# Residual of group 0 loaded by range, two pools exchanged, and head 0's operands on GpSimd's queue

## The chip, the cores and the metric

One core of a Trainium2 chip. The time is the device time of one execution in microseconds (us). Engines: TensorE (PE; its weight loads PEld), VectorE (DVE), ScalarE (ACT), GpSimd (POOL) and SyncE (SP), which here only issues DMAs. ACT and POOL can issue DMAs too, each in its own instruction order.

## The reference

One layer of a hybrid encoder for two requests, a prompt of 1024 rows and a sample of 32 rows, with the same weights (1056 rows together):

```python
h = x * (1 + sc1) + sh1                      # sc, sh, g: adaLN, silu(c) @ w_ada
mq, mk, mv, mo, mi, mf, fq, fk, fv, ff, gu, gv = split(h @ w_in)
hm = head_norm(mlstm(mq, mk, mv, mi, mf)) * norm_g * sigmoid(mo)     # 4 heads
hf = forgetting_attention(fq, fk, fv, log_sigmoid(ff))               # FoX, 8 heads
hg = gu * spatial_gate(layer_norm(gv))                               # gMLP
mix = concat([hm, hf, hg]) @ w_o
x = layer_norm(ALPHA * x + (1 + g1) * mix)
h = x * (1 + sc2) + sh2
y = (silu(h @ w_gate) * (h @ w_up)) @ w_down
x = layer_norm(ALPHA * x + (1 + g2) * y)
```

Outputs are x for both requests and the new states, the keys and values of the attention among them.

## The kernel before

The 1056 rows lie on the free axis (feature-major) and are worked in two groups: group 0 is rows 0 to 511, group 1 the other 544. Every fp32 product is made of three matmuls of a split operand: high times high (L116), high times low (L117), low times high (L118). A weight of 128 x 1024 comes in by SP as `raw` (512 KB, three buffers), ACT copies its high part (`whi`, L104), and DVE subtracts to get the low part (`wlo`, L105). `load` (L84) issues on SP and remembers the instruction as `lastload`; `store` issues on SP unless it is told another engine.

The instructions are written out in Python in one order, and a scheduler that simulates the engines then sets the order on each engine. Pools are stacks at two ends of SBUF; when one is closed, what is opened over its space waits, tile by tile, for the last reader of the old tile. `issue_after` holds what is issued in it behind an instruction that is named.

The order of work around the change, in `run`:

1. `wo_mix(0)` loads and splits the mixed heads of group 0 (`tm_ah`, `tm_al`), with feature-major units (`fm_unit`) for some heads of group 1 in between. Such a unit computes a head's queries and keys, stores them in DRAM (`start_dqh`, `start_dql`), and stores the keys as an output (`o_kT<-fm_qkr`), the last of them from ACT's queue.
2. `wo_res(0)` allocates `z0`, group 0's residual (in the trace `wo_z`), and loads it in four loads of 512 KB.
3. `wo_range` makes the output projection for rows 0 to 255 (range 0), then for rows 256 to 511 (range 1); for each block m of 128 features there are one weight and 24 matmuls 256 wide, after which DVE adds the product to `z0` (L1066). Range 1 is woven with `ln1` of range 0, and `ln1` of range 1 follows. `ln1` normalises `z0` in place on DVE, ACT writes the modulated value, and copy and difference (L1091, L1092) overwrite `tm_ah` and `tm_al`, the operands of the up projection.
4. `fm_unit` for the last heads; `ln1_res(0)` (L1094, POOL L1101) scales `z0` once more for the second residual: 16 instructions 128 x 256.
5. The stack `s1` with the pools `p1` (operands h1 of the input projection) and `sm` (small tiles, `fm_qkr` among them) is closed, and `mx1` is opened over their space for the mixers of group 1: `fox` for heads 0 to 7 (with k1, k2, qp, q2, v loaded by SP, L747 to L755) and `mlstm` units. The mLSTM unit loads `mqk`, `mqb`, `mv1`, `mo`, `mb`; ACT makes the sigmoid of `mo` in three steps (L607 to L609) and POOL multiplies it (L610); DVE and ACT make the weights `mw` from `mb` (L615, L618).
6. `up` (gate and up projection with silu, L1139 to L1145) of group 0, woven with the mixers, and `ada` (the adaLN product of a block of w_ada in four columns of PE, a copy `ada_adas` on ACT at L181, and two transposes of it on PE at L184).

Of the kernel before, what the change touches and what calls it, by code (L numbers as in the profile page):

```python
# [7 lines left out]
F32 = mybir.dt.float32  # L8
# [7 lines left out]
P = 128  # L16
D = 1024
KT = 8
# [5 lines left out]
GO = (0, 512)  # L24
GN = (512, 544)
QD = 2
MM = (((0, 256), (256, 512)), ((0, 272), (272, 544)))
# [36 lines left out]
def f(ap):  # L64
    return ap.bitcast(F32)


class Kernel:
# [12 lines left out]
        kw = {} if bufs is None else {"bufs": bufs}  # L81
        return pool.tile(shape, dt, tag=tag, name=f"{self.phase}_{tag}_{self.n}", **kw)

    def load(self, out, in_):  # L84
        self.lastload = self.nc.sync.dma_start(out, in_)
        return self.lastload

# [290 lines left out]
                    nc.gpsimd.tensor_copy(self.qks[:, h, :], kr[:, n - NS:n])  # L378
        return evac

    def decay(self, out, h, rows, tiles):
        j0, j1 = tiles
        self.load(f(out).rearrange("p (j q) -> p j q", q=P),
                  self.dfs.rearrange("(j h) r q -> h r j q", h=8)[h, rows, j0:j1])

    def head_tiles(self, h, nq, nk):
        b = self.foxbufs
# [349 lines left out]
    def fox(self, h, chunks):  # L737
        self.phase = "fox"
        mx = self.mx
        q0, q1 = chunks[0][0] * P, (chunks[-1][-1] + 1) * P  # L740
        nq, nk, nb = q1 - q0, q1, q1 // P
        if h in self.heads:
            k1, k2, qp, q2, v = self.heads.pop(h)
        else:
            k1, k2, qp, q2, v = self.head_tiles(h, nq, nk)
            qs = slice(q0, q1)
            self.load(f(qp[0:64]), self.dqh[h, 0:64, qs])  # L747
            self.load(f(qp[64:128]), self.dql[h, 0:64, qs])
            self.load(f(k1[0:64]), self.dqh[h, 64:128, :nk])
            self.load(f(k1[64:128]), self.dqh[h, 64:128, :nk])  # L750
            self.load(f(q2[0:64]), self.dqh[h, 0:64, qs])
            self.decay(q2[64:68], h, slice(2, 6), (chunks[0][0], nb))
            self.load(f(k2[0:64]), self.dql[h, 64:128, :nk])
            self.decay(k2[64:68], h, slice(0, 4), (0, nb))
            self.load(f(v), self.dv[:, :nb, h * P:(h + 1) * P])  # L755
        for tiles in chunks:
            o = tiles[0] * P - q0
            n = len(tiles) * P
            yield from self.fox_chunk(h, tiles, nk, n, k1, k2, qp[:, o:o + n], q2[:, o:o + n], v)
# [251 lines left out]
                nc.scalar.copy(h, r)  # L1011
                nc.vector.tensor_tensor(self.hl[c][a][:, k, :b - a], r, f(h), ALU.subtract)

    def wo_res(self, c, pool):
        z = self.z[c] = self.t(pool, [P, KT, GN[c]], F32, f"z{c}", 1)
        for k in range(0, KT, 2):
            self.load(z[:, k:k + 2], self.d["xT"][k:k + 2, :, GO[c]:GO[c] + GN[c]].rearrange("k p n -> p k n"))

    def wo(self, c, st, cuts, eng, res=None):
        self.phase = f"wo{c}"  # L1020
# [22 lines left out]
    def wo_range(self, st, a, b, order, kept, pool):  # L1043
        nc, ko = self.nc, self.KORDER[0]
        hh, hl = self.hh[0][a], self.hl[0][a]
        st["order"] = order
        for m in order:
            self.phase = "wo0"
            w = kept.get(m) or self.weights(self.d["w_o"][m], KT, P, None, pool if m < 3 else None)
            kept[m] = w  # L1050
            ps = self.t(self.pg, [P, 512], F32, "g")
            self.gemm(ps[:, :b - a], [w[k] for k in ko], slice(0, P), lambda i: hh[:, ko[i], :b - a],
                      lambda i: hl[:, ko[i], :b - a])
            self.sublayer_end(0, self.z[0], m, ps, "g1", st, a, b)
            yield
# [109 lines left out]
    def sup_operand(self, ks):  # L1165
# [7 lines left out]
        def load(k):  # L1173
# [5 lines left out]
            return x, y  # L1179

        loaded = {k: load(k) for k in ks[:2]}
        yield
        for k in ks:
            self.phase = "sup"
            x, y = loaded.pop(k)
            tt(y[:, b], y[:, b], x[:, b], ALU.subtract)
            tt(x[:, b], x[:, a], x[:, b], ALU.subtract)
            tt(x[:, a], y[:, b], x[:, a], ALU.add)
            tt(y[:, a], x[:, a], y[:, a], ALU.subtract)
            for z, (h, l) in zip((x, y), self.T):  # L1190
                nc.scalar.copy(h[:, k], z)
                tt(l[:, k], z, f(h[:, k]), ALU.subtract)
            if k + 2 in ks:
                loaded[k + 2] = load(k + 2)
            yield
# [141 lines left out]
    def run(self):  # L1337
        nc, tc, d = self.nc, self.tc, self.d
# [25 lines left out]
        self.constants()  # L1364
        self.ph = self.pool("ph")
        s1 = ExitStack()
        self.p1 = self.pool("p1", ctx=s1, side="right")
        self.sm = self.pool("sm", 2, ctx=s1, side="right")
        self.h1t = [self.wide_tiles(), [self.t(self.p1, [P, KT, GN[1]], F32R, x) for x in ("h1h", "h1l")]]
        self.hs = self.t(self.p1, [P, KT, 2 * NS], F32R, "hs")  # L1370
        self.G = self.t(self.p1, [P, 9, 16], F32, "G")
# [84 lines left out]
        for h in range(QD, PRE):  # L1456
            self.fm_unit(w3[2 + h], self.evac_qk(h), (1,))
        self.wo_mix(0, self.KORDER[0][6:])
        self.wo_res(0, self.pz)
        self.pn = self.pool("pn")  # L1460
        self.ln_consts()
        st = self.ln_begin(nc.vector)
# [6 lines left out]
        weave(self.ln1(0, st, *MM[0][1]))  # L1469
        for h in range(PRE, 8):  # L1470
            self.fm_unit(w3[2 + h], self.evac_qk(h, True), (1,))
        self.ln1_res(0)
        s1.close()
        s4 = ExitStack()
        self.mx = self.pool("mx1", ctx=s4, side="right")
        self.foxbufs = (2, 1, 1, 1, 2)
        self.mixers()
        s5 = ExitStack()
        pa = self.pool("pa0", ctx=s5)
        self.pu, self.utag = self.pg, "gg"  # L1480
# [74 lines left out]
        n = nj * 256  # L1555
# [3 lines left out]
        for half, (a, b) in enumerate(LN[1][::-1]):  # L1559
# [6 lines left out]
            else:  # L1566
                h, l = (self.t(pb, [P, KT * 272], F32R, f"{x}{a}", 1) for x in ("ah", "al"))
# [117 lines left out]
```

## Time and profile before

| | |
|---|---|
| time, median of 3 runs | 1366.96 us (1365.69 to 1368.74) |
| the profiled execution | 1366.61 us, span 1364.7 us, mean granted clock 0.995 |
| PE busy | 1330.3 us, 97% of the span |
| DVE, ACT, POOL busy | 995.4, 656.7, 226.6 us |
| DMA | 221.70 MB, mean 162 GB/s |

The span runs from the first to the last instruction of the trace; the profiled execution's own time is 1.9 us longer. A row of the timeline gives start, duration, engine, source line, operation, the tiles as out<-in with their buffer numbers left out, the number of instructions in the row, and in brackets the idle time before them and what ended it. A row of the list of waits gives the time waited in total, how often, and the longest. A row of the windows gives the length of the stretch, busy time and instructions of PE, PEld, DVE, ACT and POOL, then the granted clock of PE, the busy share of the DMA engines and the GB/s.

### The profile page before, as it was taken

To read this page: it belongs to the slowest core of one execution; us is meant where nothing else is said; L and a number is where in the kernel's file an instruction comes from. 1 tells how busy PE (TensorE), PEld (TensorE's weight loads), DVE (VectorE), ACT (ScalarE), POOL (GpSimd) and SP (SyncE) were. 2 spreads that over 40 slices of the span, in tenths; PEclk is the share of its full clock that TensorE was granted. 3 is DMA by queue.
4 is the path that set the end of the run, shared out by engine and by line. 5 is a ranking of instruction groups with operands and counts; after the bars stand their busy time and mean duration, and the time that the engine had idled before them with its cause. 6 is when DMAs were issued, how large, how long until landed. Compare 5 with 4: busy or idle time off the path is not lost.

```text
span 1364.7 us, 25185 instructions
## 1 busy us (share of the span) xinstructions
PE 1330.3 (97%) x9434; PEld 1215.8 (89%) x9434; DVE 995.4 (73%) x2129; ACT 656.7 (48%) x1306; POOL 226.6 (17%) x263
## 2 busy tenths in 40 slices
PE   7999999999999899999999999999999999999996
PEld 4898889998989777888887888999999999999995
DVE  5545553679769667786776765678988988879777
ACT  3314454545536554545545354336664554645355
POOL 0202000053134200000000000373710000000341
PEclk9999999999999899999999999999999999999998
DMA  9765565547454765454344334574596758454321
GB/s 359 273 231 152 161 206 154 163 138 212 134 201 135 207 189 171 119 154 134 109 122 120 104 110 130 156 181 124 164 254 170 205 149 223 146 170 127 99 79 66
DMA packets 119289, 221.70 MB, mean 162 GB/s; under 512 B 18676, under 2 KB 62352, under 8 KB 119168
## 3 DMA queue, kind: packets, MB, share of 16 engines
q1 hardware_dynamic: 111936, 207.55, 48.9%
q0 software_dynamic: 6032, 11.94, 5.1%
q8 instruction: 74, 1.21, 0.4%
q10 hardware_dynamic: 1200, 0.62, 0.2%
q14 instruction: 47, 0.39, 0.1%
HBM read 188.13 MB, written 51.85 MB: 176 GB/s over the span
## 4 chain that ended last, share of the span: by engine, by line
PE 84%; DVE 7%; DMA 5%; ACT 2%; issue 1%; SPq 1%; POOL 1%; DVEq 0%; ACTq 0%
PE up_g L117 5%; PE up_g L118 5%; PE up_g L116 5%; PE dn_g L116 4%; PE dn_g L118 4%; PE dn_g L117 4%; PE tm_g L281 3%; PE tm_g L282 3%; PE tm_g L283 3%; PE sup_u L118 3%; PE sup_u L116 3%; PE sup_u L117 3%; PE fox_t L815 2%; PE sup_g L117 2%; PE sup_g L118 2%; PE sup_g L116 2%
## 5 line engine op out<-in xcount | busy, mean ns | idle before, releaser
L117 PE MATMUL up_g<-tm_al,up_whi 128*128 128x512 f32 (+1 forms) x384 | 141.0, 367 | 0.5 <-DVE tm_al L1092 0.5
L116 PE MATMUL up_g<-tm_ah,up_whi 128*128 128x512 f32 (+1 forms) x384 | 141.2, 369 | 0.2
L118 PE MATMUL up_g<-tm_ah,up_wlo 128*128 128x512 f32 (+1 forms) x384 | 140.5, 366 | 0.0
L1211 ACT CAST sup_whi<-sup_raw 128x1024 fp32r<-128x1024 f32 x54 | 56.0, 1048 | 90.3 <-PE dn_u L117 46.7
L116 PEld LDWEIGHTS up_g<-tm_ah,up_whi 128*128 128x128 f32 x384 | 72.7, 190 | 12.5 <-ACT tm_ah L1091 0.6
L117 PEld LDWEIGHTS up_g<-tm_al,up_whi 128*128 128x128 f32 x384 | 73.1, 190 | 11.1 <-DVE tm_al L1092 0.7
L118 PEld LDWEIGHTS up_g<-tm_ah,up_wlo 128*128 128x128 f32 x384 | 73.2, 191 | 10.7
L788 ACT ACTIVATE fox_p<-fox_s,fox_fmx 128x384 f32<-128x384 f32 (+2 forms) x96 | 55.1, 578 | 44.8 <-DVE fox_fmx L786 37.4
L104 ACT CAST up_whi<-up_raw 128x1024 fp32r<-128x1024 f32 x50 | 52.4, 1048 | 49.7 <-PE up_g L117 19.0
L1212 DVE TENSOR_TENSOR sup_wlo<-sup_raw,sup_whi 128x1024 fp32r<-128x1024 f32 x54 | 68.2, 1267 | 10.5 <-ACT sup_whi L1211 10.5
L1066 DVE SCALAR_TENSOR_TENSOR wo_z<-dn_g,start_mod,wo_z 128x512 f32<-128x512 f32 (+4 forms) x120 | 60.3, 521 | 20.1 <-PE dn_g L118 19.7
L105 DVE TENSOR_TENSOR up_wlo<-up_raw,up_whi 128x1024 fp32r<-128x1024 f32 x50 | 65.7, 1314 | 11.6 <-ACT up_whi L104 11.0
L116 PE MATMUL dn_g<-up_acth,dn_whi 128*128 128x512 f32 (+2 forms) x200 | 74.1, 371 | 0.0
L118 PE MATMUL dn_g<-up_acth,dn_wlo 128*128 128x512 f32 (+2 forms) x200 | 73.4, 367 | 0.0
L117 PE MATMUL dn_g<-up_actl,dn_whi 128*128 128x512 f32 (+2 forms) x200 | 72.9, 365 | 0.0
L820 ACT CAST fox_pth<-fox_t 128x512 fp32r<-128x512 f32 (+1 forms) x80 | 41.0, 545 | 59.5 <-PE fox_t L815 59.3
L104 ACT CAST dn_whi<-dn_raw 128x1024 fp32r<-128x1024 f32 (+1 forms) x44 | 42.7, 971 | 52.2 <-PE up_g L117 10.7
L783 DVE TENSOR_REDUCE fox_fmx<-fox_s 128x1 f32<-128x384 f32 (+2 forms) x96 | 52.7, 553 | 13.0 <-PE fox_s L780 11.8
L821 DVE TENSOR_TENSOR fox_ptl<-fox_t,fox_pth 128x512 fp32r<-128x512 f32 (+1 forms) x80 | 49.5, 631 | 14.5 <-ACT fox_pth L820 14.4
L105 DVE TENSOR_TENSOR dn_wlo<-dn_raw,dn_whi 128x1024 fp32r<-128x1024 f32 (+1 forms) x44 | 49.5, 1125 | 13.7 <-ACT dn_whi L104 13.2
L281 PE MATMUL tm_g<-tm_whi,start_h1h 128*128 128x256 f32 (+1 forms) x192 | 55.3, 288 | 1.7 <-ACT tm_vhl L711 1.7
L282 PE MATMUL tm_g<-tm_wlo,start_h1h 128*128 128x256 f32 (+1 forms) x192 | 55.1, 287 | 0.0
(667 smaller groups left out, 4806.8 us busy)
## 6 DMA issues: line engine op xcount, KB each, us to landing
up_raw<-w_gu SPq DMA_DIRECT2D x50, 512.0 KB
dn_raw<-w_dn SPq DMA_DIRECT2D x28, 512.0 KB
ada_late<-w_ada SPq DMA_DIRECT2D x24, 512.0 KB
sup_raw<-w_gu SPq DMA_DIRECT2D x20, 512.0 KB
start_dp<-w_gu SPq DMA_DIRECT2D x19, 512.0 KB
start_dp<-w_gu POOLq DMA_DIRECT2D x19, 512.0 KB, 7.5
wo_raw<-w_o SPq DMA_DIRECT2D x18, 512.0 KB
sup_raw<-start_dp SPq DMA_DIRECT2D x18, 512.0 KB
```

What stands on the lines that cost most here:

```text
L104: nc.scalar.copy(hi[:, :w], raw[:, :w])
L105: (eng or nc.vector).tensor_tensor(lo[:, :w], raw[:, :w], f(hi[:, :w]), ALU.subtract)
L116: nc.tensor.matmul(ps, hi, xh(k), start=start and k == 0, stop=False)
L117: nc.tensor.matmul(ps, hi, xl(k), start=False, stop=False)
L118: nc.tensor.matmul(ps, lo, xh(k), start=False, stop=stop and k == n - 1)
L281: nc.tensor.matmul(ps[:, :ncol], xh, hi, start=k == 0, stop=False)
L282: nc.tensor.matmul(ps[:, :ncol], xh, lo, start=False, stop=False)
L783: nc.vector.tensor_reduce(mxs[:, x:x + 1], s[:, :w], AX.X, ALU.max, negate=True)
L788: nc.scalar.activation(pr[:, lo:hi], banks[x][:, :hi - lo], AF.Exp, bias=mxs[:, 0:1], accum_out=sums[:, x:x + 1])
L1066: self.lastz = self.nc.vector.scalar_tensor_tensor(z[:, m, x:y], ps[:, x - a:y - a], g[i], z[:, m, x:y], ALU.mult, ALU.add)
L1211: nc.scalar.copy(h, x)
L1212: tt(l, x, f(h), ALU.subtract)
```

## The change

Four edits:

1. `wo_res` loads two blocks of one range (256 KB). For range 0 it is called just ahead of the weights of m = 0, 2, 4, 6; the four halves of range 1 are issued at m = 5 and m = 7, behind the weight that was loaded last. `z0` is allocated where it was.
2. `sm` and `p1` change places in the stack, so that head 0's k1, k2, qp, q2 and v lie over `p1`'s tiles, and mLSTM's tiles over those of `sm`.
3. Head 0's loads of qp, k1, q2 and k2 (eight DMAs) are issued by GpSimd; the last is remembered as `lastside`. v stays on SP.
4. `ln1_res(0)` is issued after `mixers()`, behind `lastside`.

```diff
-    def load(self, out, in_):
+    def load(self, out, in_, eng=None):
+        if eng:
+            self.lastside = eng.dma_start(out, in_)
+            return self.lastside
         self.lastload = self.nc.sync.dma_start(out, in_)
         return self.lastload
...
+            eng = self.nc.gpsimd if h == 0 else None
+            self.load(f(qp[0:64]), self.dqh[h, 0:64, qs], eng)
...
+            self.decay(k2[64:68], h, slice(0, 4), (0, nb), eng)
             self.load(f(v), self.dv[:, :nb, h * P:(h + 1) * P])
...
-    def wo_res(self, c, pool):
-        z = self.z[c] = self.t(pool, [P, KT, GN[c]], F32, f"z{c}", 1)
-        for k in range(0, KT, 2):
-            self.load(z[:, k:k + 2], self.d["xT"][k:k + 2, :, GO[c]:GO[c] + GN[c]].rearrange("k p n -> p k n"))
+    def wo_res(self, a, b, k):
+        self.load(self.z[0][:, k:k + 2, a:b], self.d["xT"][k:k + 2, :, a:b].rearrange("k p n -> p k n"))
...
             self.phase = "wo0"
+            if a == 0 and m % 2 == 0:
+                self.wo_res(a, b, m)
             w = kept.get(m) or self.weights(self.d["w_o"][m], KT, P, None, pool if m < 3 else None)
+            if a == 0 and m in (5, 7):
+                with self.tc.issue_after(self.lastload.ins):
+                    for k in ((0, 4), (6, 2))[m // 7]:
+                        self.wo_res(*MM[0][1], k)
...
+        self.sm = self.pool("sm", 2, ctx=s1, side="right")
         self.p1 = self.pool("p1", ctx=s1, side="right")
-        self.sm = self.pool("sm", 2, ctx=s1, side="right")
...
-        self.wo_res(0, self.pz)
+        self.z[0] = self.t(self.pz, [P, KT, GN[0]], F32, "z0", 1)
...
-        self.ln1_res(0)
         s1.close()
         s4 = ExitStack()
         self.mx = self.pool("mx1", ctx=s4, side="right")
         self.foxbufs = (2, 1, 1, 1, 2)
         self.mixers()
+        with tc.issue_after(self.lastside.ins):
+            self.ln1_res(0)
```

The change lengthens the file, so lines of after are 3 to 8 higher (L104 is L107 there, L181 is L184, L607 is L610, L779 is L783, L1101 is L1109).

SP's queue at the output projection, before: the residual `wo_z` in four loads, then the weights `wo_raw` of m = 3 and on (those of m = 0 to 2 were issued earlier), with stores of a feature-major unit between.

```order
L85 DMA wo_z_895_4890<-xT 128x2x512 x4
L85 DMA wo_raw_5023<-w_o 128x1024
L85 DMA wo_raw_5060<-w_o 128x1024
L89 DMA start_dqh_57<-fm_qkh_4840 128x272
L85 DMA wo_raw_5097<-w_o 128x1024
L89 DMA start_dqh_57<-fm_qkh_4874 128x272
L89 DMA start_dql_58<-fm_qkl_4841 128x272
L89 DMA start_dql_58<-fm_qkl_4875 128x272
L85 DMA wo_raw_5134<-w_o 128x1024
L85 DMA wo_raw_5171<-w_o 128x1024
```

The same place in the changed kernel:

```order
L88 DMA wo_z_895_4890<-xT 128x2x256 x2
L88 DMA wo_raw_5021<-w_o 128x1024
L88 DMA wo_z_895_4890<-xT 128x2x256
L88 DMA wo_raw_5059<-w_o 128x1024
L88 DMA wo_z_895_4890<-xT 128x2x256
L92 DMA start_dqh_57<-fm_qkh_4840 128x272
L88 DMA wo_raw_5096<-w_o 128x1024
L88 DMA wo_z_895_4890<-xT 128x2x256
L92 DMA start_dqh_57<-fm_qkh_4874 128x272
L92 DMA start_dql_58<-fm_qkl_4841 128x272
L88 DMA wo_z_895_4890<-xT 128x2x256
L92 DMA start_dql_58<-fm_qkl_4875 128x272
```

The first weight has two loads of 256 KB ahead of it instead of four of 512 KB, and the rest of the residual stands between and behind the weights.

SP's queue at the start of group 1's mixers, in the changed kernel, behind the last weight that up loads before them (`up_raw`); in before, the loads of qp, k1, q2 and k2 stand between `up_raw` and `fox_v`, and `mlstm_mqb` ahead of `mlstm_mv`.

```order
L88 DMA up_raw_7991<-w_gu 128x1024
L88 DMA fox_v_5829<-start_dv_59 128x8x128
L88 DMA foxs_k_1071_6020<-cache_k 64x1024
L88 DMA mlstm_mqk_6148<-start_dmqk_60 128x4x128
L88 DMA mlstm_mv_1103_6154<-start_dmv_61 128x4x64
L88 DMA foxs_k_1071_6020<-start_dsf_65 1x4x256
L88 DMA mlstm_mo_6157<-start_dmo_62 128x256
L88 DMA mlstm_mb_6159<-start_dM_66 128x512
```

Those eight loads went to POOL, and in the changed kernel it is `mlstm_mv` that has to wait for the last reader of a tile of `sm`, the store `o_kT<-fm_qkr`; in before it was `fox_qp`.

ACT's order at that place, before: behind the last copies of `ln1` come the adaLN copy, a weight of up, the silu of up's first block (`up_sil`), the softmax of head 0 (`fox_p`), and only then the mLSTM unit.

```order
L1091 COPY tm_ah_4639<-lna_tmp_5587 128x256
L181 COPY ada_adas_7970<-ada_g_7957 128x256
L104 COPY up_whi_7989<-up_raw_7987 128x1024
L1139 ACTIVATE up_sil_7892<-up_g_7900 128x256
L1140 ACTIVATE up_sil_7892<-up_sil_7892,start_ones_36_112 128x256
L1141 ACTIVATE up_sil_7892<-up_sil_7892 128x256
L788 ACTIVATE fox_p_5853,fox_fsm_5852<-fox_s_5854,fox_fmx_5851 128x384
L788 ACTIVATE fox_p_5853,fox_fsm_5852<-fox_s_5858,fox_fmx_5851 128x256
L607 ACTIVATE mlstm_mo_6169<-mlstm_mo_6169 128x256
```

The same place in the changed kernel:

```order
L1099 COPY tm_ah_4639<-lna_tmp_5591 128x256
L610 ACTIVATE mlstm_mo_6157<-mlstm_mo_6157 128x256
L611 ACTIVATE mlstm_mo_6157<-mlstm_mo_6157,start_ones_36_112 128x256
L107 COPY up_whi_7993<-up_raw_7991 128x1024
L1147 ACTIVATE up_sil_7896<-up_g_7904 128x256
L612 ACTIVATE mlstm_mo_6157<-mlstm_mo_6157 128x256
L621 ACTIVATE mlstm_mw_6196<-mlstm_mw_6196,start_col_178 128x128 x4
L1148 ACTIVATE up_sil_7896<-up_sil_7896,start_ones_36_112 128x256
L184 COPY ada_adas_7974<-ada_g_7961 128x256
L1149 ACTIVATE up_sil_7896<-up_sil_7896 128x256
```

The mLSTM unit's instructions moved ahead of the adaLN copy and into the silu of up's first block. On PE the order moved with it: in before 16 of the 96 matmuls of that block and the two adaLN transposes stood behind head 0's first score matmuls (L779); now all 96 stand ahead of them, the transposes right behind, and then the first 512-wide matmul of the next block.

More of the change, by code (lines that the diff above doesn't have):

```diff
@@ L379, in evac_qk, with decay @@
         return evac
-    def decay(self, out, h, rows, tiles):
+    def decay(self, out, h, rows, tiles, eng=None):
         j0, j1 = tiles
         self.load(f(out).rearrange("p (j q) -> p j q", q=P),
-                  self.dfs.rearrange("(j h) r q -> h r j q", h=8)[h, rows, j0:j1])
+                  self.dfs.rearrange("(j h) r q -> h r j q", h=8)[h, rows, j0:j1], eng)
     def head_tiles(self, h, nq, nk):
@@ L746, in fox @@
             qs = slice(q0, q1)
[L747 to L754, printed above, removed]
+            eng = self.nc.gpsimd if h == 0 else None
+            self.load(f(qp[0:64]), self.dqh[h, 0:64, qs], eng)
+            self.load(f(qp[64:128]), self.dql[h, 0:64, qs], eng)
+            self.load(f(k1[0:64]), self.dqh[h, 64:128, :nk], eng)
+            self.load(f(k1[64:128]), self.dqh[h, 64:128, :nk], eng)
+            self.load(f(q2[0:64]), self.dqh[h, 0:64, qs], eng)
+            self.decay(q2[64:68], h, slice(2, 6), (chunks[0][0], nb), eng)
+            self.load(f(k2[0:64]), self.dql[h, 64:128, :nk], eng)
+            self.decay(k2[64:68], h, slice(0, 4), (0, nb), eng)
             self.load(f(v), self.dv[:, :nb, h * P:(h + 1) * P])
```

## The prediction

> **What bounds the kernel now.** I read the page's busy shares first, then the list of waits of TensorE (PE), then the timeline at the two places where PE waits inside the stretch that the change touches.
>
> ```profile
> PE 1330.3 (97%) x9434; PEld 1215.8 (89%) x9434; DVE 995.4 (73%) x2129; ACT 656.7 (48%) x1306; POOL 226.6 (17%) x263
> ...
> PE fox_s L779 <- DMA fox_k<-start_dqh: 4.2, 1, 4.2
> ...
> PE wo_g L116 <- ACT tm_ah L1003: 1.2, 1, 1.2
> PE wo_g L118 <- DVE wo_wlo L105: 1.1, 2, 0.8
> ...
> PE wo_g L116 <- ACT wo_whi L104: 0.6, 1, 0.6
> ```
>
> PE is busy 97% of the span, so only what PE waits for can be won. In reach of the change are two places: head 0's first score matmul (L779, 4.2 us, waiting for k1) and the first output-projection range (the `wo_g` rows, 2.9 us together).
>
> ```profile
> 456.70 0.28 PE L116 MATMUL up_g<-tm_ah,up_whi 128*128 128x256 f32 x1
> 461.21 0.87 PE L779 MATMUL fox_s<-fox_k,fox_qp 128*128 128x384 f32 x2 [4.23 <-DMA fox_k<-start_dqh]
> ...
> 466.21 0.40 PE L116 MATMUL up_g<-tm_ah,up_whi 128*128 128x512 f32 x1
> ...
> 459.00:460.00 1.00, 0.00 (x0) 0.00 (x0) 0.00 (x0) 0.00 (x0) 0.00 (x0) 0.65 1.00 234
> 460.00:466.00 6.00, 4.79 (x21) 4.82 (x22) 0.54 (x3) 0.68 (x1) 0.00 (x0) 0.50 1.05 214
> 466.00:467.00 1.00, 1.00 (x6) 0.87 (x6) 0.72 (x3) 0.97 (x3) 0.00 (x0) 0.93 1.22 245
> ```
>
> The stall costs more than its 4.23 us. The granted clock (the column behind the five engines) falls to 0.65 in 459 to 460, about 2.7 us after the last matmul ended, and is 0.50 until 466. PE's 4.79 busy us there are worth half at full clock: another 2.4 us. **Head 0 costs 6.6 us in all.**
>
> Why k1 is late is seen in SyncE's queue (SP).
>
> ```profile
> 449.94 0.48 ACTq L89 DMA_DIRECT2D o_kT<-fm_qkr  x1
> ...
> 450.02 0.33 SPq L85 DMA_DIRECT2D up_raw<-w_gu  x1
> 454.06 0.47 SPq L85 DMA_DIRECT2D fox_qp<-start_dqh  x1
> ...
> 456.27 1.18 SPq L85 DMA_DIRECT2D fox_k<-start_dqh  x2
> ...
> SPq L85 <- DMA o_kT<-fm_qkr: 3.4, 1, 3.4
> ```
>
> SP stood 3.4 us, until 454.06, for the last `o_kT` store to land, because qp lies over tiles of pool sm that this store reads. k1 went out at 456.27 and landed 4 to 5 us later.
>
> **The first term: the residual's loads.** Group 0's residual, 2 MB, is issued ahead of three weights of w_o.
>
> ```profile
> 371.34 3.41 SPq L85 DMA_DIRECT2D wo_z<-xT  x4
> 374.85 1.42 SPq L85 DMA_DIRECT2D wo_raw<-w_o  x2
> ...
> 384.01 1.05 ACT L104 CAST wo_whi<-wo_raw 128x1024 fp32r<-128x1024 f32 x1 [5.68 <-DMA wo_raw<-w_o]
> ...
> 384.26 0.28 PE L118 MATMUL wo_g<-tm_ah,wo_wlo 128*128 128x256 f32 x1
> 385.11 0.38 PE L116 MATMUL wo_g<-tm_ah,wo_whi 128*128 128x256 f32 x1 [0.57 <-ACT wo_whi L104]
> ...
> 386.37 0.39 PE L118 MATMUL wo_g<-tm_ah,wo_wlo 128*128 128x256 f32 x1 [0.76 <-DVE wo_wlo L105]
> 386.59 0.28 PE L116 MATMUL wo_g<-tm_ah,wo_whi 128*128 128x256 f32 x1
> ...
> 370.00:380.00 10.00, 8.82 (x73) 8.61 (x72) 6.45 (x8) 4.23 (x7) 3.21 (x6) 1.00 0.89 292
> 380.00:390.00 10.00, 8.67 (x69) 8.16 (x69) 4.97 (x7) 4.47 (x7) 3.95 (x6) 1.00 0.89 319
> 400.00:410.00 10.00, 10.00 (x84) 9.90 (x83) 4.83 (x9) 2.44 (x5) 1.56 (x2) 1.00 0.11 42
> ```
>
> ACT waited 5.68 us for the fourth weight (m=3), and PE twice for what ACT and VectorE (DVE) make of it. At the steps of 0.12 us before, the matmul of 386.59 would have started at 384.26 + 4 x 0.12 = 384.7, so 1.9 us were lost. Now 0.5 MB of the residual lies ahead of that weight instead of 2 MB. At the 300 GB/s of these windows 1.5 MB are 5 us, more than the 1.9 us needed: **-1.9 us**. The later halves go out among later weights, where the queues have slack (DMA share 0.11 in 400 to 410). The 1.2 us wait on `tm_ah` needs the last mix load, which stays ahead of the residual; I take nothing for it. Bounds: 0 (a half delays the next weight as much) to -3.1 us. Nothing on PE waits between there and head 0, and DVE is only half busy in 400 to 410, so I take it that all engines move ahead together.
>
> **The second term: head 0.** The eight loads now stand in GpSimd's queue (POOL), behind the last feature-major matmul.
>
> ```profile
> 444.50 0.29 PE L118 MATMUL fm_g<-start_h1h,fm_wlo 128*128 128x272 f32 x1
> ...
> 370.56 0.54 POOL L89 DMA_DIRECT2D o_kT<-fm_qkr  x1 [0.29 <-POOL fm_qkr L370]
> ...
> o_kT<-fm_qkr POOLq DMA_DIRECT2D x10, 68.0 KB, 4.7
> ...
> 448.63 4.90 POOL L1101 TENSOR_SCALAR wo_z<-wo_z,start_colp 128x256 f32<-128x256 f32 x3 [12.27 <-ACT lna_tmp L1087]
> ...
> 454.02 3.78 POOL L1101 TENSOR_SCALAR wo_z<-wo_z,start_colp 128x256 f32<-128x256 f32 x5
> ```
>
> I use before's clock times and take the 1.9 us off at the end. Eight issues of 0.54 us from 444.8 end at 449.1; with 4.7 us to land, the last are there by 454. PE needs them when its 256-wide up matmuls are done; the order puts the 16 that stood behind the score matmuls ahead of them: 456.98 + 16 x 0.12 = 458.9, plus 0.3 for the two score matmuls, 459.2. So **the old wait is gone**: -4.2 us, and -2.4 us of half clock if no other wait follows.
>
> One does. The wait for the `o_kT` store did not vanish with the exchange of pools: mLSTM's tiles now lie over sm, and in SP's order `mlstm_mv` waits for it, with `mlstm_mo` and `mlstm_mb` behind. In ACT's order the sigmoid of `mlstm_mo` stands ahead of `up_whi`, the silu of up's first block, `mlstm_mw` and `ada_adas`. For `ada_adas` PE waits (its transposes stand right behind head 0's score matmuls), and for the silu, since the next 512-wide gate needs that PSUM bank. In before, ACT did `ada_adas` at 456.06 and waited for `mlstm_mo` only far behind.
>
> ```profile
> 456.06 0.36 ACT L181 COPY ada_adas<-ada_g 128x256 f32<-128x256 f32 x1
> 465.32 1.05 ACT L104 CAST up_whi<-up_raw 128x1024 fp32r<-128x1024 f32 x1 [8.89 <-PE up_g L117]
> 466.27 0.38 ACT L1139 ACTIVATE up_sil<-up_g 128x256 f32<-128x256 f32 x1
> 466.68 0.51 ACT L1140 ACTIVATE up_sil<-up_sil,start_ones 128x256 f32<-128x256 f32 x1
> ...
> 470.03 0.41 ACT L607 ACTIVATE mlstm_mo<-mlstm_mo 128x256 f32<-128x256 f32 x1
> ...
> 471.04 1.27 ACT L618 ACTIVATE mlstm_mw<-mlstm_mw,start_col 128x128 f32<-128x128 f32 x4
> ...
> 459.68 0.57 SPq L85 DMA_DIRECT2D fox_v<-start_dv  x1
> ...
> 466.11 0.33 SPq L85 DMA_DIRECT2D mlstm_mb<-start_dM  x1
> ...
> 470.02 0.69 DVE L615 TENSOR_TENSOR mlstm_mw<-mlstm_mb,start_maskbig 128x512 f32<-128x512 f32 x1 [0.66 <-DMA mlstm_mb<-start_dM]
> ```
>
> The store lands at 454.06 as before; POOL's two memsets take about 0.6 us, and `mlstm_mv`, a small load and `mlstm_mo` follow at some 0.6 us each, so `mlstm_mo` goes out at about 455.9. Before, `mlstm_mb` took 3.9 us to be used; I take 4 us: it is there at T = 459.9. Then ACT does, in its new order, 0.41 + 0.51 for mo, 1.05 for `up_whi`, 0.38 (silu), 0.41 (mo), 1.27 (`mlstm_mw`), 0.51 (silu), 0.36 (`ada_adas`); as they overlap by about 0.1 us each that is 4.5 us, and PE's transposes start at 464.4. The last silu step and DVE's product (0.42 and 0.41) add 0.6 us before the gate starts, at 465.2. PE idles 5.2 + 0.6 = 5.8 us where it idled 4.2, and the clock falls again, which I price as before, 2.4 us. **Head 0 then costs 8.2 us instead of 6.6: +1.6 us.** Bounds on T: 457.9 (2 us to land) gives a gain of 0.4 us here; 463 (below) a loss of 4.7 us.
>
> On the clock the Trainium skill ("TensorE: Matmul & The Clock Gate", Part 1) says that an idle window of about 3.4 us halves it and that as long a busy one restores it. By that rule a wait below 3.4 us, which an early T gives, may cost nothing more; by the row, which shows 0.65 after 2.7 us, it could. The sum takes the row.
>
> **Other edits.** ln1_res moves on POOL behind the loads: 16 instructions, 0.76 us each where DVE is quiet, so it ends some 10 us later than before and holds mo's product on POOL as long. Its result is read only far behind, in the down projection's residual; the product's readers are mLSTM's output steps, behind the first fox blocks. I cost both at 0, at most +1 us. The freed SP issues (8 x 0.55 us) bring later loads forward; worth 0 to -0.5, taken 0.
>
> **Sum** against the profiled execution (1366.61 us; span 1364.7 and 1.9 around it, 0.35 below the median 1366.96): -1.9 + 1.6 = -0.3, **1366.3 us**: no change. A measurement of this kernel tells about 0.2% (2.7 us) from no change.
>
> **Rivals.**
> A. *The wait simply goes.* `mlstm_mo` lands early or ACT is not held by it, and PE runs through: -6.6 - 1.9 = -8.5 us, 1358.1. With a short wait under the clock's patience (T near 457.5: PE idles about 3.4 us in all, no half clock) -0.8 - 2.4 - 1.9 = -5.1, 1361.5. For it: SP's queue is 4 us shorter and the store lands at 454.06, well ahead of PE's need at 459.2. Against it: every load of this stretch took about 4 us to land, and ACT has 4.5 us to do behind mo. Chance 0.28, from 1358 to 1363.5.
>
> B. *The wait grows: slower.* GpSimd's 1.2 MB and `fox_v` are now in flight while the last `o_kT` store lands. In before its 68 KB took 4 us (449.94 to 454.06) beside little traffic, while between `fox_v` at 459.68 and `mlstm_mb` at 470.02 some 1.6 MB took 10.3 us. If the store lands 2 us later and mo takes 5 us, T = 463, the gate starts at 468.3, and head 0 costs 8.9 + 2.4 = 11.3 us: +4.7 - 1.9 = +2.8 us, 1369.4; with another us on either, 1371. It decides from T = 463 on. Chance 0.24.
>
> C. *GpSimd's queue is starved.* DVE is all but full here, and POOL's three instructions at 448.63 took 1.6 us each where the five at 454.02 took 0.76. If issues stretch by the same 2.1, eight take 9.1 us and end at 454; k1, the fourth, lands by 455 plus some. Even if POOL issued nothing before DVE falls quiet at 457, k1 would go out by 459.2 and land by 463.9, ahead of the 464.4 that `ada_adas` gives: 1366.3 again, since the new wait covers it; but it takes rival A away (1366 instead of 1358). Beside it stands a rule of the Trainium skill ("SBUF — State Buffer", "SBUF: two separate sides"), which speaks against this edit: a DMA issued by GpSimd cannot write its descriptors while DVE holds the shared port, and belongs on another queue. The stretched POOL rows agree with a held port; no row here shows an issue stretched. Chance 0.06.
>
> D. *The residual's halves do nothing* (the loads queue up as before): -0.3 + 1.9 = +1.6, 1368.2. Chance 0.06.
>
> **How the numbers follow.** The forecast, a new wait of about the same price, has 0.36 and its own range 1363.5 to 1369; A 0.28, B 0.24, C 0.06, D 0.06. Faster by over 0.2% is A and a little of the forecast (0.05): 0.33. Slower is B: 0.24. The rest, 0.43, is within 0.2%. The range 1360 to 1371 leaves out half of A (0.14) and the far end of B (0.05).
>
> **What would show it.** Right: `fox_s` (L783) without a DMA wait; in its place a PE wait of 3 to 6 us on `ada_adas` L184, ACT idle until `mlstm_mo` just ahead, SP's wait for `o_kT` on `mlstm_mv`; PEclk 0.50 for some 6 us around it; no wait on `wo_whi` and `wo_wlo` at m=3. Wrong: no PE wait over 2 us between 450 and 470 (A); `mlstm_mo` landing 13 us or more after the last `o_kT` store is issued (B); GpSimd's eight issues taking over 1 us each (C); the waits at m=3 still there (D).

## The result, and the profile after

The change made the kernel slower by 0.33%.

| | before | changed |
|---|---|---|
| median (19 runs each) | 1366.87 us | 1371.3 us |
| ratio | | 1.0033, 95% interval 1.0025 to 1.0042 |
| span of the profiled execution | 1364.7 us | 1369.2 us |

PE's list of waits in the changed kernel has a new first row:

```profile
PE ada_g L187 <- ACT ada_adas L184: 7.2, 1, 7.2
...
PE wo_g L119 <- ACT tm_ah L1007: 0.8, 1, 0.8
PE wo_g L119 <- ACT wo_qs L940: 0.8, 1, 0.8
...
PE up_g L119 <- DVE up_sil L1150: 0.7, 1, 0.7
PE up_g L120 <- DVE tm_al L1100: 0.6, 1, 0.6
```

Head 0's wait for k1 (4.2 us) is gone, and so are the waits on `wo_wlo` and `wo_whi`. In their place PE waits 7.2 us for `ada_adas`. The timeline at that place:

```profile
442.76 0.29 PE L121 MATMUL fm_g<-start_h1h,fm_wlo 128*128 128x272 f32 x1
443.35 0.55 POOL L86 DMA_DIRECT2D fox_qp<-start_dqh  x1 [28.83 <-PE fm_g L121]
447.08 0.64 POOL L86 DMA_DIRECT2D fox_k<-start_dfs  x1
448.21 0.49 ACTq L92 DMA_DIRECT2D o_kT<-fm_qkr  x1
448.76 0.69 SPq L88 DMA_DIRECT2D fox_v<-start_dv  x1
453.87 0.38 SPq L88 DMA_DIRECT2D mlstm_mv<-start_dmv  x1
455.06 0.42 SPq L88 DMA_DIRECT2D mlstm_mo<-start_dmo  x1
455.53 0.43 SPq L88 DMA_DIRECT2D mlstm_mb<-start_dM  x1
458.08 0.55 PE L783 MATMUL fox_s<-fox_k,fox_qp 128*128 128x384 f32 x2
461.52 0.42 ACT L610 ACTIVATE mlstm_mo<-mlstm_mo 128x256 f32<-128x256 f32 x1 [7.09 <-issue]
462.24 0.93 DVE L618 TENSOR_TENSOR mlstm_mw<-mlstm_mb,start_maskbig 128x512 f32<-128x512 f32 x1 [7.30 <-DMA mlstm_mb<-start_dM]
465.47 0.35 ACT L184 COPY ada_adas<-ada_g 128x256 f32<-128x256 f32 x1
465.87 0.69 PE L187 MATMUL ada_g<-start_ident,ada_adas 128*128 128x128 f32 x2 [7.24 <-ACT ada_adas L184]
466.65 0.79 PE L119 MATMUL up_g<-tm_ah,up_whi 128*128 128x512 f32 x1
```

Read from the end: PE's transposes start at 465.87, when ACT has copied `ada_adas`; ACT comes to it 4 us after `mlstm_mo` is there; `mlstm_mo` was issued at 455.06, behind `mlstm_mv`, which stood until the last `o_kT` store had landed (the sixteenth and last update of the store's semaphore came at 453.79; SyncE's list of waits names ACT's `tm_ah`, whose semaphore came 0.03 us later). DVE stands in the same way, 7.30 us, for `mlstm_mb`. ("issue" in ACT's row means that the profile shows no releaser; the instruction's semaphores are those of the `mlstm_mo` load.)

The same stretch in windows (PE, PEld, DVE, ACT, POOL, then granted clock, DMA share, GB/s):

```profile
450.00:456.00 6.00, 5.27 (x43) 4.32 (x43) 4.13 (x11) 4.43 (x13) 1.89 (x5) 1.00 1.09 261
456.00:459.00 3.00, 2.63 (x24) 1.83 (x22) 0.00 (x0) 0.00 (x0) 3.00 (x6) 1.00 1.16 186
459.00:461.00 2.00, 0.00 (x0) 0.00 (x0) 0.00 (x0) 0.00 (x0) 2.00 (x5) 0.82 1.11 331
461.00:466.00 5.00, 0.13 (x1) 0.13 (x2) 2.16 (x2) 4.45 (x12) 4.16 (x6) 0.50 0.77 258
466.00:470.00 4.00, 3.91 (x10) 2.83 (x11) 1.79 (x7) 0.57 (x3) 0.00 (x0) 0.50 0.61 238
```

PE, DVE and ACT all stand from 459 to 461 while the DMA engines are full (share above 1.0 from 450 to 461; a packet's whole time is counted where it starts, so the share can pass 1.0), and PE then works at half clock until 470.5.

Where the 4.5 us of span came from can be counted. I gave each PE matmul the time until the next one starts and took off the median of its kind (the same tile and shapes); what is left is waiting, half clock and the changes between kinds. From the first `wo_g` to the last `fm_g` this excess fell from 5.75 to 3.59 us (**-2.2**). From there to head 0's scores it grew from 2.6 to 3.7 (**+1.1**). At head 0 and until the clock is back it grew from 6.7 to 10.0 (**+3.3**). In the 50 us behind, from 5.4 to 7.9 (**+2.5**), 1.8 of it because PE goes to the short adaLN matmuls and back more often (seven times instead of three, for 48 matmuls in both). Behind that, until group 1's output projection, it is -0.5. The sum is +4.2; the remaining 0.3 lies outside these stretches.

### The profile page after: what moved, and what is told of

It is laid out like the page before. It is cut to its first block, busy times and chain, and to the rows that moved or that the text cites. A ratio compares the mean times of both kernels' runs of the same rounds, so it can differ in the third digit from the quotient of the medians.

```text
span 1369.2 us, 25209 instructions
## 1 busy us (share of the span) xinstructions
PE 1333.5 (97%) x9434; PEld 1215.4 (89%) x9434; DVE 998.5 (73%) x2129; ACT 657.0 (48%) x1306; POOL 223.4 (16%) x271
## 4 chain that ended last, share of the span: by engine, by line
PE 88%; DMA 4%; DVE 4%; ACT 2%; issue 1%; SPq 1%; ACTq 0%; DVEq 0%
PE up_g L119 6%; PE up_g L120 6%; PE up_g L121 6%; PE dn_g L119 4%; PE dn_g L121 4%; PE dn_g L120 4%; PE tm_g L284 3%; PE tm_g L285 3%; PE tm_g L286 3%; PE sup_u L121 3%; PE sup_u L119 3%; PE sup_u L120 3%; PE fox_t L819 2%; PE wo_g L119 2%; PE wo_g L120 2%; PE wo_g L121 2%
## 5 line engine op out<-in xcount | busy, mean ns | idle before, releaser
L107 ACT CAST up_whi<-up_raw 128x1024 fp32r<-128x1024 f32 x50 | 52.4, 1048 | 50.5 <-PE up_g L120 16.7
L107 ACT CAST dn_whi<-dn_raw 128x1024 fp32r<-128x1024 f32 (+1 forms) x44 | 42.7, 971 | 47.8 <-PE dn_u L120 10.8
```

Source lines behind the costliest of these rows:

```text
L107: nc.scalar.copy(hi[:, :w], raw[:, :w])
```

## The experiments

Times are medians on one chip beside its own runs of the kernel before, and ratios have their 95% interval. Clock times of different executions differ by up to 2 us at the place where the change begins, so waits are compared and not starts.

**The first edit alone, in the kernel before.**

```diff
-        self.wo_res(0, self.pz)
+        self.z[0] = self.t(self.pz, [P, KT, GN[0]], F32, "z0", 1)
...
+            if a == 0 and m % 2 == 0:
+                self.wo_res(a, b, m)
```

(and the halves of range 1 at m = 5 and 7, as in the change)

> Kernel before with the first edit alone (residual by range). Theory: the third-row weight of range 0 comes 4 to 5 us earlier, the waits on wo_whi and wo_wlo at m=3 go, and everything behind keeps that lead: 2 us less than before, 1364.9 (0.9985). In the trace of the changed kernel PE stood 2.15 us further at 430 than in before, but lost 0.9 of it by 455 to waits on VectorE and ScalarE; if that loss belongs to the first edit, 1.2 us less, 1365.7. Rival (the halves do nothing, since head 0 waits for a store that comes when it comes): 1366.9, 1.000.

Measured: 1364.7 us beside 1367.18, ratio 0.9982 (0.9966 to 0.9999). The theory held, though the interval ends just below the rival's 1.000 and takes in both of the theory's numbers. Its profile also shows head 0 better off, though nothing was changed there:

```profile
448.99 0.47 ACTq L89 DMA_DIRECT2D o_kT<-fm_qkr  x1
451.10 0.47 SPq L85 DMA_DIRECT2D fox_qp<-start_dqh  x1
458.45 0.56 PE L779 MATMUL fox_s<-fox_k,fox_qp 128*128 128x384 f32 x2 [2.40 <-DMA fox_k<-start_dqh]
```

SyncE was free of the store about 2 us after its issue here, 4.1 us in before, 5.7 us in the changed kernel (448.21 to 453.87). Why it took 4.1 us in before is not shown; `up_raw` was issued 0.08 us behind the store there, 0.36 us here.

**The changed kernel without the first edit.**

```diff
-            if a == 0 and m % 2 == 0:
-                self.wo_res(a, b, m)
...
+        self.wo_res(0, self.pz)
```

> Changed kernel without its first edit: the residual of group 0 in four loads ahead of the weights again. The other three edits alone. Theory (the first edit is worth about 2 us wherever the rest is): waits on wo_whi and wo_wlo at m=3 are back, 1371.3 + 2 = 1373.3 (1.0048). Rival (its lead is lost on the way to head 0, where PE waits for loads anyway): 1371.3 (1.0033).

Measured: 1374.78 us beside 1366.14, ratio 1.0061 (1.0049 to 1.0073). The theory held: PE waits 1.1 us for `wo_wlo` and 0.4 us for `wo_whi` again. The first edit is worth 0.0028 of 1366 us there, 3.8 us, and some 2 to 6 us with the intervals of the two ratios. The harm lies in the other three edits together.

**ScalarE freed of the mLSTM unit.** In the changed kernel:

```diff
+        with self.tc.issue_after(self.foxp.ins) if j == 4 else ExitStack():
+            nc.scalar.activation(mo[:L], mo[:L], AF.Exp, scale=-1.0)
...
-                nc.scalar.activation(pr[:, lo:hi], banks[x][:, :hi - lo], AF.Exp, bias=mxs[:, 0:1],
+                self.foxp = nc.scalar.activation(pr[:, lo:hi], banks[x][:, :hi - lo], AF.Exp, bias=mxs[:, 0:1],
```

(the lines that make `mw` stand in the same kind of block)

> Changed kernel, with ScalarE's three sigmoid steps of the first mLSTM unit of group 1, and the exponentials of its mw with the DVE sum ahead of them, issued behind head 0's first softmax; loads and queues stay as they are. Theory (ScalarE stands in its order behind mlstm_mo, and PE behind ScalarE): the wait of 7.2 us on ada_adas, the 0.7 us at the next gate and some 2 us of half clock go: 1371.3 - 10 = 1361 (0.996 of before). Rival (the loads crowd each other, and PE only meets the next late one): a wait of several us on head 0's score matmuls or on a weight of up in its place, 1367 or more.

Measured: 1370.31 us beside 1367.18, ratio 1.0022 (1.001 to 1.0035). The theory's 1361 did not come. The time lies in the rival's range, but PE met neither of the waits that the rival named; the profile says why:

```profile
458.57 0.37 ACT L184 COPY ada_adas<-ada_g 128x256 f32<-128x256 f32 x1
462.17 0.75 DVE L620 TENSOR_TENSOR mlstm_mw<-mlstm_mb,start_maskbig 128x512 f32<-128x512 f32 x1 [6.84 <-DMA mlstm_mb<-start_dM]
464.33 0.41 DVE L1152 TENSOR_TENSOR up_sil<-up_g,up_sil 128x256 f32<-128x256 f32 x1
464.80 0.79 PE L119 MATMUL up_g<-tm_ah,up_whi 128*128 128x512 f32 x1 [5.36 <-DVE up_sil L1152]
...
PE wo_g L119 <- ACT up_ah L1017: 1.3, 1, 1.3
```

`ada_adas` was made at 458.57 and PE no longer waited for it. But the order was constrained on ACT alone (and behind head 1's first softmax, which was issued last when the unit is written), and DVE still stood behind `mlstm_mb` until 462.17. PE waited 5.4 us for DVE's silu product instead: one late pair of loads, two engines behind it, and the second wait was hidden under the first. That is not all of it. By the count of excess above, this kernel lost some 5.7 us less than the changed kernel between the first `wo_g` and 600 us, and some 2.7 us more behind that. Most of those 2.7 us lie in group 1's output projection, near 880 and 898, where PE waited 1.3 us for `up_ah` (the last row) and 1.0 us for `wo_z`; neither before nor the changed kernel has these waits, and what made them is not shown.

**Both engines freed.** As above, with one more block for DVE, both behind head 0's first block:

```diff
+        with self.tc.issue_after(self.foxp.ins) if j == 4 else ExitStack(), self.tc.issue_after(self.foxd.ins) if j == 4 else ExitStack():
...
+                if self.first0 and x == 1:
+                    self.foxd = red
```

> Changed kernel, with the first mLSTM unit's work on mo and mb issued behind head 0's first softmax on ScalarE and behind head 0's first maxima on VectorE; the loads stay. In the second experiment ScalarE was freed and VectorE still stood behind mlstm_mb until 462, so PE waited 5.4 us for VectorE instead of 7.2 us for ScalarE. Theory (PE waits because two engines stand, in their order, behind two late loads): with both freed nothing on PE waits over 1 us in 455 to 470 and the clock stays up: 1371.3 - 7.2 - 0.7 - 2.1 = 1361 (0.996). Rival (the loads of this stretch are too many, and the next late one stops PE: q2, k2 or a weight of up): a wait of 3 us or more, 1366 or more.

Measured: 1364.23 us beside 1366.14, ratio 0.9987 (0.9975 to 0.9999). The theory held for the wait: nothing on PE waits over 0.7 us between 440 and 470, and the clock stays at 1.00.

```profile
459.00:461.00 2.00, 1.68 (x7) 1.41 (x8) 1.89 (x7) 0.41 (x1) 2.00 (x4) 1.00 0.99 312
461.00:466.00 5.00, 5.00 (x23) 4.04 (x23) 0.00 (x0) 0.00 (x0) 3.59 (x7) 1.00 0.80 226
```

For the time it was too low by 3 us (the execution that was profiled took 1366.11, 1.9 us above the median). PE, which by the columns it had streamed stood about 6 us further than in before at 470, ran into the next block:

```profile
462.97 9.76 SPq L89 DMA_DIRECT2D up_raw<-w_gu  x2
470.07 1.05 ACT L108 CAST up_whi<-up_raw 128x1024 fp32r<-128x1024 f32 x1 [9.90 <-DMA up_raw<-w_gu]
473.80 0.50 PE L120 MATMUL up_g<-tm_ah,up_whi 128*128 128x512 f32 x1 [1.76 <-DVE up_sil L1157]
493.88 0.79 PE L786 MATMUL fox_s<-fox_k,fox_qp 128*128 128x512 f32 x1 [2.03 <-ACT fox_p L797]
```

ACT stood 9.9 us, now for a weight of up; the silu behind it held PE at 473.80, and a softmax held PE at 493.88. By 500 the lead over before was 0.3 us. So even without a wait over 0.7 us at head 0 most of the gain is given back within 30 us, in smaller waits than the rival's 3 us.

**Head 0's loads back on SyncE's queue.**

```diff
-            eng = self.nc.gpsimd if h == 0 else None
+            eng = self.nc.sync if h == 0 else None
```

> Changed kernel, with head 0's eight loads back on SyncE's queue; the pools stay exchanged, the residual goes by range. The order of this kernel has ada_adas and the silu ahead of mlstm_mo on ScalarE, as in before. Theory (the harm is that emptying SyncE's queue let mLSTM move ahead on ScalarE; the exchange of pools alone frees head 0 of the store): the loads go out from 449 at 0.6 us each, k1 is there by 456 to 457, PE waits for nothing or below 1 us: 1358 to 1361. Rival (the queue itself was the gain, and on SyncE k1 is late as before): a wait of 2 to 4 us on head 0's score matmul, 1364 to 1367.

Measured: 1366.15 us beside 1367.18, ratio 0.9988 (0.9972 to 1.0005). With this line alone undone the loss is gone, but the theory's 1358 to 1361 did not come: the time is the rival's. The wait lies between the two, since PE waited 1.3 us for k1 instead of 4.2, and the clock stayed at 1.00 until 501. By the columns it had streamed PE stood 5 us further than in before at 470 and 0.5 us at 500, after waits of 0.4 to 1.1 us for weights of up and for DVE in the attention blocks; the gain is given back as with both engines freed. With the eight loads ahead of them in the same queue, the mLSTM loads stand later in the planner's order, and ACT's order has `ada_adas` and the silu ahead of `mlstm_mo` again.

```profile
455.93 0.36 ACT L184 COPY ada_adas<-ada_g 128x256 f32<-128x256 f32 x1
466.60 0.42 ACT L610 ACTIVATE mlstm_mo<-mlstm_mo 128x256 f32<-128x256 f32 x1 [1.65 <-DMA mlstm_mqb<-start_dmqk]
```

`mlstm_mo` is used at 466.6 here, later than in the changed kernel, and PE does not wait for it. That it is late is harmless; that two engines stand behind it is not.

**The pools in their old places.**

```diff
-        self.sm = self.pool("sm", 2, ctx=s1, side="right")
         self.p1 = self.pool("p1", ctx=s1, side="right")
+        self.sm = self.pool("sm", 2, ctx=s1, side="right")
```

> Changed kernel with the two pools in their old places; head 0's loads on GpSimd, residual by range, ScalarE's order as in the changed kernel. Theory (mlstm_mo is late because it stands behind a load that waits for the last o_kT store): mlstm_mo now goes out near 452 and is used near 458 instead of 461.5; head 0's loads wait for the store on GpSimd instead, k1 goes out near 455.5 and lands near 460.5, so PE waits 2 to 3 us there and then about 1 to 2 us for ada_adas: 1365 to 1367. Rival (mlstm_mo is late because of the bytes ahead of it): still used after 460, PE waits about 7 us on ada_adas: 1370 to 1373.

Measured: 1375.11 us beside 1367.18, ratio 1.0049 (1.0026 to 1.0073). Four of the eight runs took 1369.70 to 1372.70 us, the rival's range or just below it, and four 1377.52 to 1378.53; the profile is of one of the upper four. The theory was wrong. `mlstm_mv` no longer waited for the store, and `mlstm_mo` went out at 454.58; but it was used at 467.77:

```profile
452.74 0.55 POOL L86 DMA_DIRECT2D fox_qp<-start_dqh  x1 [36.59 <-ACT tm_ah L1099]
454.58 0.43 SPq L88 DMA_DIRECT2D mlstm_mo<-start_dmo  x1
465.01 0.87 PE L783 MATMUL fox_s<-fox_k,fox_qp 128*128 128x384 f32 x2 [3.76 <-DMA fox_k<-start_dqh]
467.77 0.42 ACT L610 ACTIVATE mlstm_mo<-mlstm_mo 128x256 f32<-128x256 f32 x1 [11.70 <-DMA mlstm_mo<-start_dmo]
472.13 0.69 PE L187 MATMUL ada_g<-start_ident,ada_adas 128*128 128x128 f32 x2 [6.25 <-ACT ada_adas L184]
```

The rows of the queues between 459 and 465 (packets, MB, share of the 16 engines; q0 is GpSimd's, q1 SyncE's):

```profile
q0 software_dynamic: 381, 1.07, 79.0%
q1 hardware_dynamic: 536, 0.30, 26.0%
```

GpSimd's 1.1 MB moved ahead of SyncE's transfers that were issued just before or with it: by the updates of their semaphores `mlstm_mv`, issued at 452.48, landed at 467.56, and `fox_qp`, issued by GpSimd at 452.74, at 461.57. `mlstm_mo` took 13 us, and PE waited twice, for k1 and for `ada_adas`.

**mo and mb loaded first.** In the changed kernel:

```diff
+        self.pre[self.nextm] = self.mlstm_pre(self.nextm, P)
         for h in range(8):
...
-        mo = t([P, 256], "mo", 1)
-        self.load(mo[:L], self.dmo[:L, j, :])
+        mo, mb = self.pre.pop(j, None) or self.mlstm_pre(j, L)
```

> Changed kernel, with mo and mb of that mLSTM unit loaded ahead of fox_v on SyncE's queue, as the first loads of the mixers; ScalarE's order has the sigmoid steps among the last copies of ln1. Theory A (they were late because of the bytes ahead of them, and because GpSimd's loads hold the DMA engines from 446 to 451 whatever SyncE has issued): issued near 449, used near 453 to 455, so that the last tm_ah copies are delayed by 0 to 2 us and ada_adas by nothing: 1361 to 1364. Theory B (they lie over tiles of the pool sm and wait for the last o_kT store, wherever they stand): SyncE stands until 454 with fox_v and all else behind it, mo is used near 457 to 458, tm_ah late with it: 1367 or more.

Measured: 1365.54 us beside 1366.14, ratio 0.9992 (0.9981 to 1.0004). Theory A: issued at 448.09, before `mlstm_mv`'s wait, mo was used at 454.07, the wait on `ada_adas` was gone, and PE waited 1.5 us for `tm_ah`. The time is 1.5 us above the range that A gave and cannot be told from before; the profile has 1.6 us of PE waiting for `up_ah` in group 1's output projection, where before has none.

```profile
448.09 0.60 SPq L89 DMA_DIRECT2D mlstm_mo<-start_dmo  x1
448.74 0.42 SPq L89 DMA_DIRECT2D mlstm_mb<-start_dM  x1
454.07 0.42 ACT L616 ACTIVATE mlstm_mo<-mlstm_mo 128x256 f32<-128x256 f32 x1 [2.21 <-DMA mlstm_mo<-start_dmo]
454.88 0.81 DVE L624 TENSOR_TENSOR mlstm_mw<-mlstm_mb,start_maskbig 128x512 f32<-128x512 f32 x1 [2.23 <-DMA mlstm_mb<-start_dM]
456.52 0.38 PE L120 MATMUL up_g<-tm_ah,up_whi 128*128 128x256 f32 x1 [1.50 <-ACT tm_ah L1105]
```

**The same, with nothing on GpSimd's queue.** The kernel above with `eng = self.nc.sync if h == 0 else None`.

> The kernel of e6 with head 0's eight loads on SyncE's queue behind mo and mb, nothing of it on GpSimd; pools exchanged, residual by range. In e6 mo was issued at 448.1 and used at 454.1, 6 us, while GpSimd's loads ran from 444 to 451. Theory (GpSimd's loads hold the DMA engines, and SyncE's transfers go behind them even when they are first in their own queue): without them mo is used 3 to 4 us after its issue. Rival (the transfers of this stretch take 6 us anyway): 5 us or more again. For the time: k1 goes out 1.3 us later than in e3, where PE waited 1.3 us for it, so PE waits 2 to 3 us for k1 and nothing for ScalarE: 1364 to 1367 (0.997 to 1.000).

Measured: 1364.64 us beside 1366.66, ratio 0.9982 (0.9973 to 0.9992), inside the range that was expected. PE waited 1.4 us for k1, where 2 to 3 were expected, nothing for ScalarE at head 0, and 1.2 us for DVE's `tm_al`.

```profile
450.71 0.58 SPq L89 DMA_DIRECT2D mlstm_mo<-start_dmo  x1
451.34 0.48 SPq L89 DMA_DIRECT2D mlstm_mb<-start_dM  x1
455.28 0.42 ACT L616 ACTIVATE mlstm_mo<-mlstm_mo 128x256 f32<-128x256 f32 x1
457.29 0.69 DVE L624 TENSOR_TENSOR mlstm_mw<-mlstm_mb,start_maskbig 128x512 f32<-128x512 f32 x1 [1.53 <-DMA mlstm_mb<-start_dM]
```

mo was used 4.6 us after its issue, but ACT was busy until then. By the updates of their semaphores mo landed 4.3 us after its issue (455.05), against 6.0 us with GpSimd's loads in flight (448.09 to 454.05), and mb 5.9 us after its issue, against 6.1. In both kernels a weight of up (`up_raw`) stands ahead in SyncE's queue. So for mo the truth lies between the theory and the rival, with some 1.6 us for GpSimd's loads, and for mb the rival holds.

**ln1_res at its old place.**

```diff
+        self.ln1_res(0)
         s1.close()
...
-        with tc.issue_after(self.lastside.ins):
-            self.ln1_res(0)
```

> Changed kernel, with ln1_res(0) issued ahead of the mixers again, as in before; GpSimd then does eleven of its sixteen instructions ahead of head 0's loads. Theory (the place of ln1_res costs nothing by itself; what matters is when head 0's loads go out): the loads go out behind the normalised rows, some 5 to 8 us later than in the changed kernel, so that head 0's scores wait several us: 1373 to 1377. Rival (ln1_res behind the loads is what delays mLSTM's product and PE): 1368 or less.

Measured: 1377.88 us beside 1366.14, ratio 1.0083 (1.0062 to 1.0104). The theory held in its mechanism: head 0's first load went out at 452.83 instead of 443.35, 9.5 us later where 5 to 8 were expected, and PE waited 5.9 us for k1 and 2.0 us for `ada_adas`. The time is 0.9 us above its range. The place of ln1_res in the change is not what harms; with the loads on GpSimd's queue it has to be there.

## Why the prediction was wrong

Its range ended at 1371.0, and the time was 1371.3; it forecast no change, and the ratio's interval lies above 1. The mechanism was the one forecast, a new wait on `ada_adas` in place of the old one on k1, and three steps failed by their size: the time T at which `mlstm_mo` is there, the lead that all engines were to keep, and what the edits do behind head 0, which was taken at 0. By the count of excess they are worth 1.7, 1.1 and 2.5 us, and the last, which the forecast did not have, is the largest.

- **The residual's loads: right.** Forecast -1.9 us; measured -2.2 up to the last `fm_g`, and 2.5 us (with head 0's shorter wait in it) and 3.8 us in the two experiments.
- **"I take it that all engines move ahead together": wrong by about 1 us.** PE came to the 256-wide up matmuls 1.7 us earlier, and met DVE there, twice: 0.6 us for `tm_al` and 0.7 for `up_sil`, where before showed 0.5 once. The prediction took DVE as half busy from 400 to 410; in before it was busy 19.97 of the 20 us behind that, and 9.50 of the 10 us from 440 to 450.
- **The old wait is gone: right.** The score matmuls ran at 458.08 without a wait. GpSimd's loads took up to 6.5 us to land instead of 4.7, the last at 453.58, which was still early enough.
- **T, the time at which `mlstm_mo` is there: the step that failed in the wait itself.** The forecast, with its 1.9 us taken off, has mo issued at 454.0 and used at 458.0. It was issued at 455.06 and used at 461.52: 1.1 us late at the store's wait, and 6.5 us to land instead of "I take 4 us". The 4 us came from one load that was issued when the burst before it had partly gone. Here SyncE's own loads were still ahead of it. By the updates of their semaphores the last of GpSimd's loads had landed at 453.58, and SyncE's landed in the order of their issue: `up_raw` 454.68, `fox_v` 457.82, `foxs_k` from `cache_k` 459.18, `mlstm_mqk` 459.64, `mlstm_mv` 461.10, `mlstm_mo` 461.45. The queues from 455.06 to 461.45 (packets, MB, share of the 16 engines):

```profile
q1 hardware_dynamic: 2282, 1.55, 112.6%
```

There is no row of GpSimd's queue (q0) in that stretch. This is rival B (more in flight around the last store); it was given 0.24, and T = 461.5 + 1.9 = 463.4 lies past its point of 463, where its price was +2.8 us. Its sign came too: mo landed 13.2 us after the store was issued.
- **From T on: right.** ACT's chain took 4.35 us to the transposes (forecast 4.5), and 0.78 us more to the gate (0.8 with the transposes). The clock: 0.50 until 470.5 costs half of the 3.91 us that PE was busy before 470, 2.0, and a little behind; forecast 2.4. With the idle time, head 0 cost 10.0 us where 8.2 was forecast, and 6.7 before. T was 3.5 us late, but PE came to its wait 1.3 us late too.
- **"Other edits ... taken 0": wrong by about 2 us.** In the 50 us behind head 0 PE goes to the short adaLN matmuls seven times instead of three, 1.8 us more in all; the prediction has no price for their order. It is the planner's order and not the loads alone: the kernel with ScalarE freed has the same loads and queues, and goes there three times.
- Rival A, the wait that simply goes, was shown to be out of reach in another way than the prediction has it: the kernel with both engines freed has no wait over 0.7 us at head 0 and is 1.9 us faster than before, not 8.5, since the next weights are late for a PE that comes 6 us early.
- Rival C, starving of GpSimd's queue by DVE, did not happen. The eight issues took 4.4 us (443.35 to 447.72), 0.55 us each, in a stretch where DVE was nearly full. The Trainium skill's rule that a held port keeps GpSimd from writing descriptors ("SBUF — State Buffer", "SBUF: two separate sides") shows in none of these rows. Whether DVE held the port there is not shown.

GpSimd's loads did their harm ahead of mo's issue. In the five kernels in which GpSimd had issued them before the last `up_raw` ahead of the mixers, that `up_raw` took 6.0 to 6.6 us to land and the last `o_kT` store 5.3 to 6.7; in the six others 3.7 to 5.1 us and 2.0 us (4.0 in before). What stays open is how much earlier mo would have landed if this start alone had been undone; no run keeps everything else as it is.

## What to carry to other kernels

Emptying a queue does more than bring its loads forward: a planner that sees them earlier will put their consumers earlier into the in-order engines, and a load that was harmlessly late then stops every engine that stands behind it. Before an edit of this kind, look at which instructions moved ahead of the critical ones, whether they wait for a load, and what the loads' time to land is when all of them come at once. The residual alone (0.9982) or mo first on SyncE (0.9982) beat both kernels; the change as a whole did not.

## What the runs showed of the hardware

The TensorE clock fell after shorter waits than rival A of the prediction allowed for (about 3.4 us in all). In the kernel with the residual alone, PE waited 2.40 us at one place, and the windows around it show

```profile
456.00:459.00 3.00, 0.60 (x5) 0.56 (x5) 0.29 (x1) 0.00 (x0) 1.17 (x2) 1.00 0.87 218
459.00:461.00 2.00, 2.00 (x16) 2.00 (x15) 0.00 (x0) 0.00 (x0) 0.00 (x0) 0.72 1.13 250
461.00:466.00 5.00, 5.00 (x21) 4.31 (x21) 3.61 (x11) 3.14 (x7) 0.00 (x0) 0.77 0.88 202
```

that the clock dropped after PE had started again at 458.45. The trace's record of the clock has it at half from 459.87 to 463.29, 3.41 us, and PE had been busy 1.43 of the 3.41 us before. The ends of the kernel apart, every stretch at half clock in the eleven traces lasts 3.41 us or a whole multiple of it (6.83 in before, 10.24 in the changed kernel). The Trainium skill ("TensorE: Matmul & The Clock Gate", Part 1) gives an idle window of about 3.4 us; here 2.4 us were enough, so the row decides, and a wait below 3.4 us cannot be taken as free of a clock's fall. Nor does each such wait bring one: the 1.3 us for k1 with head 0's loads back on SyncE left the clock at 1.00 there.
